# Score products of two heads side by side in the halves of the partitions: layer 0's attention of a two-block network

## The chip, the cores and the metric

The kernel runs on one core of a Trainium2 chip. The metric is the device time of one execution in microseconds (us), lower is better; it is given as the median of several runs. Names of engines in the rows: PE is TensorE's matmuls, PEld its weight loads, DVE is VectorE, ACT is ScalarE, POOL is GpSimd, SP issues most transfers.

## What is computed

Two transformer blocks in float32 on 256 latent tokens and 256 context tokens of 1024 features. The change touches the first layer's mixer alone. It has sixteen heads of 64 features: eight of kind A (a window of 128 keys around the query, two key heads shared by four query heads each, and a sink per head in the softmax's sum) and eight of kind B (a neighbourhood on the token grid, with a learnt bias by row and column distance). Latent queries see 256 latent and 256 context keys, context queries see the 256 context keys. Cut to what matters:

```python
o_a = window_attention(qa, ka, va, ka_c, va_c, a_sink)                  # 8 heads, kind A
o_b = neighbourhood_attention(qb, kb, vb, kb_c, vb_c, b_rpb, rows_n)    # 8 heads, kind B
y_lat = concatenate([o_a, o_b]) @ w_out
oa_c = ctx_self_attention(qa_c, ka_c, va_c, scale, a_sink)              # context queries
ob_c = ctx_self_attention(qb_c, kb_c, vb_c, scale)
y_ctx = concatenate([oa_c, ob_c]) @ w_out
```

## The kernel before

Every float32 operand of a large product is kept as two parts of a shorter form, `hi` and `lo`, and a product is three matmuls (`mm3`, lines 297 to 299: hi x hi, hi x lo, lo x hi). In the rows a score product therefore has three lines: L297, L298, L299.

The queries and keys of two heads, a pair, lie transposed in one tile [128, 512]: head e of the pair has the partitions 64 e to 64 e + 63, the columns are 256 latent and 256 context tokens. A latent score product of one head and one query tile of 128 contracts over 64 partitions and streams all 512 keys; a context product streams 256.

The work of layer 0 is written as Python generators that are emitted side by side. `weave` takes at each step the generator that is least far on, measured by the sum of its yields; `lead` stretches one's sum. A scheduler then puts each engine's instructions in an order, by the order of emission and by when it expects operands to be there, and each engine works through its own list. The weaves around the change are these:

```python
self.weave(self.qkvA(), ada0(1), lead=(1.0, 1.100))
self.weave(self.chain(self.qkvB(0), self.outproj0(0)), self.chain(self.attnA(0), self.attnA(1)), ada0(2), lead=(1.0, 1.000, 1.000))
self.weave(self.qkvB(1), self.attnB(0), lead=(1.0, 1.000))
self.weave(self.outproj12(), self.attnB(1), self.lat_norm(A[0], R), lead=(2.000, 1.0, 1.000))
```

`attnA` and `attnB` each hand two pairs to `attn`. It goes through (pair, latent or context, head): `scores` of one, then `weigh` of the one before. `scores` makes the two query tiles of one head (tile `sl` for the latent, one tile `sc` with both query tiles for the context), adds the window mask (L1140) or the bias (L1142), and calls `softmax`: maxima (L1051), the negated maximum `nm` (L1053, L1055), exponentials with their sums (L1057), the sink's share (L1060, L1061), reciprocal and scaling (L1062, L1064). `weigh` transposes the probabilities (`turn`, tile `pps`, copied to `PT`) and, after the pair's second head, multiplies by the values (`values`, tile `ov`) and cuts the result into `OT`. The last `attn` has `split`: the latent parts of both pairs come first, then the context parts, and `lat_norm` begins with the latent's last out-projection as soon as the latent parts are done.

`bias(h)` fetches the bias of a head of kind B with four small transfers from POOL's queue (L1171), adds the column mask on POOL (L1173), and has two buffers `bm`.

PSUM: the pool `ps_s` has two banks (tag `s`, which `sl` and `sc` use), `ps_a` three (in-projection `ip`, out-projection `op`, most `ov`), `ps_t` two for transposes and one more, `fil`. The probabilities `Pm` are [128, 2, 512] with two buffers.

Other names in the rows: `wh` and `wl` are the parts of the weight blocks, cut from `wr` (L185, L186); `xl`, `xc` the residual streams; `qh`, `ql` the parts of q; `adaps` the modulation's products.

## Time and profile before

| what | value |
|---|---|
| median of 3 runs | 1709.74 us |
| lowest and highest | 1708.4 and 1711.4 us |
| span of the profiled execution | 1706.0 us |
| TensorE matmuls busy | 1655.3 us, 97% of the span |
| TensorE weight loads busy | 1405.4 us, 82% |
| VectorE busy | 1130.2 us, 66% |
| ScalarE busy | 715.1 us, 42% |
| GpSimd busy | 218.4 us, 13% |
| mean granted TensorE clock | 0.988 of full speed |

The profiled execution is one run under the hardware profiler; the span goes from its first to its last instruction, and the runs' median lies 3.7 us above it. Matmuls are pipelined, so the duration of one holds time in which the next has begun: what a matmul costs TensorE is read from one start to the next. Two matmuls can also run at the same time, and their busy time counts once.

### The profile page before, as it was taken

Reading aid. Unit: us, or ns where it says so; the run is one execution under the profiler, and the core shown is the slowest. Engines: PE = TensorE matmul, PEld = TensorE weight load, DVE = VectorE, ACT = ScalarE, POOL = GpSimd, SP = SyncE. Lnnn points to the kernel's source line nnn. Section 1 sums busy time; section 2 is a strip of 40 time slices with the busy share of each in tenths; the row PEclk is TensorE's granted clock in tenths of the full one; section 3 lists DMA queues with packets and bytes.
Section 4 is the critical chain, followed back from the end, with each engine's and each line's share of the span. In section 5 each row is a group of like instructions: output and inputs, shape, how many; then the busy total and the mean of one; then the engine's idle time right before and its main releaser. Section 6 shows DMA issues by size and latency. Waiting matters only on the chain.

```text
span 1706.0 us, 30446 instructions
## 1 busy us (share of the span) xinstructions
PE 1655.3 (97%) x12256; PEld 1405.4 (82%) x12256; DVE 1130.2 (66%) x2156; ACT 715.1 (42%) x1336; POOL 218.4 (13%) x294
## 2 busy tenths in 40 slices
PE   7999999999999999998999999999999999999998
PEld 5676687687877787666667999998989999899997
DVE  3575856667767776558777885675865856665643
ACT  3344443332332323147664644443533435444442
POOL 1430132110000000225321100101020000100000
PEclk8999999999999999999999999999999999999999
DMA  9684254225567777573222454454423545545652
GB/s 339 210 230 126 53 58 72 54 83 185 179 210 239 243 245 221 161 232 107 67 58 64 147 163 146 152 172 116 139 73 112 157 132 159 173 139 184 185 168 81
DMA packets 193229, 257.31 MB, mean 151 GB/s; under 512 B 9263, under 2 KB 166816, under 8 KB 193088
## 3 DMA queue, kind: packets, MB, share of 16 engines
q1 hardware_dynamic: 189488, 248.29, 46.1%
q0 software_dynamic: 2016, 2.33, 3.0%
q10 hardware_dynamic: 1584, 4.74, 0.8%
q8 instruction: 96, 1.57, 0.4%
q14 instruction: 45, 0.37, 0.1%
HBM read 254.28 MB, written 1.05 MB: 150 GB/s over the span
## 4 chain that ended last, share of the span: by engine, by line
PE 89%; DMA 4%; ACT 2%; DVE 2%; issue 1%; POOL 1%; POOLq 0%; DVEq 0%; SPq 0%; ACTq 0%
PE m L297 11%; PE m L299 11%; PE m L298 11%; PE ov L1091 3%; PE pf L297 3%; PE pf L298 3%; PE pf L299 3%; PE ip L297 2%; PE ip L298 2%; PE ip L299 2%; PE pps L1077 2%; PE adaps L508 2%; PE part L362 2%; PE ml L1534 1%; PE pg L299 1%; PE pg L297 1%
## 5 line engine op out<-in xcount | busy, mean ns | idle before, releaser
L185 ACT ACTIVATE wh<-wr 128x1024 fp32r<-128x1024 f32 (+3 forms) x354 | 332.2, 984 | 420.9 <-PE m L298 189.9
L186 DVE TENSOR_TENSOR wl<-wr,wh 128x1024 fp32r<-128x1024 f32 (+3 forms) x354 | 402.2, 1164 | 146.6 <-ACT wh L185 145.9
L299 PE MATMUL m<-hh,wl 128*128 128x256 f32 (+1 forms) x544 | 177.5, 329 | 0.5 <-DVE wl L186 0.5
L297 PE MATMUL m<-hh,wh 128*128 128x256 f32 (+1 forms) x544 | 176.7, 330 | 1.1 <-ACT hh L395 1.1
L298 PE MATMUL m<-hl,wh 128*128 128x256 f32 (+1 forms) x544 | 177.1, 328 | 0.0
L297 PE MATMUL m<-hidh,wh 128*128 128x512 f32 (+1 forms) x512 | 173.6, 341 | 0.0
L298 PE MATMUL m<-hidl,wh 128*128 128x512 f32 (+1 forms) x512 | 172.6, 338 | 0.0
L299 PE MATMUL m<-hidh,wl 128*128 128x512 f32 (+1 forms) x512 | 172.6, 338 | 0.0
L357 POOL TENSOR_TENSOR sq<-xl 128x256 f32<-128x256 f32 x48 | 31.6, 662 | 721.1 <-DVE xl L1234 692.5
L299 PEld LDWEIGHTS m<-hh,wl 128*128 128x128 f32 x544 | 103.3, 190 | 11.6 <-issue 1.9
L297 PEld LDWEIGHTS m<-hh,wh 128*128 128x128 f32 x544 | 102.3, 190 | 12.6 <-issue 1.9
L298 PEld LDWEIGHTS m<-hl,wh 128*128 128x128 f32 x544 | 103.4, 190 | 9.5 <-issue 0.8
L297 PEld LDWEIGHTS m<-hidh,wh 128*128 128x128 f32 x512 | 96.7, 190 | 15.5 <-issue 3.8
L298 PEld LDWEIGHTS m<-hidl,wh 128*128 128x128 f32 x512 | 97.1, 190 | 14.6 <-issue 4.8
L299 PEld LDWEIGHTS m<-hidh,wl 128*128 128x128 f32 x512 | 96.9, 189 | 13.3 <-issue 3.3
L297 PE MATMUL pf<-hfh,wh 128*128 128x256 f32 x352 | 99.5, 287 | 1.1 <-ACT hfh L395 1.1
L298 PE MATMUL pf<-hfl,wh 128*128 128x256 f32 x352 | 100.0, 285 | 0.0
L299 PE MATMUL pf<-hfh,wl 128*128 128x256 f32 x352 | 100.0, 285 | 0.0
L297 PE MATMUL ip<-wh,hh 128*128 128x256 f32 x288 | 86.2, 301 | 0.0
L298 PE MATMUL ip<-wl,hh 128*128 128x256 f32 x288 | 84.6, 294 | 0.2 <-DVE wl L186 0.2
L299 PE MATMUL ip<-wh,hl 128*128 128x256 f32 x288 | 83.6, 290 | 0.0
L1234 DVE SCALAR_TENSOR_TENSOR xl<-m,mod,xl 128x256 f32<-128x256 f32 x64 | 30.6, 481 | 74.3 <-PE m L299 74.2
(592 smaller groups left out, 4185.2 us busy)
## 6 DMA issues: line engine op xcount, KB each, us to landing
wr<-in_mlp_w SPq DMA_DIRECT2D x128, 512.0 KB, 4.6
av<-in_ada_w SPq DMA_DIRECT2D x48, 512.0 KB, 4.0
wr<-in_w_ffn_in SPq DMA_DIRECT2D x44, 512.0 KB, 4.6
wr<-in_w_in SPq DMA_DIRECT2D x42, 512.0 KB, 4.4
wr<-in_ada_w SPq DMA_DIRECT2D x32, 512.0 KB, 6.2
av<-in_w_mod SPq DMA_DIRECT2D x32, 512.0 KB, 4.1
wr<-in_w_gate SPq DMA_DIRECT2D x24, 512.0 KB, 4.6
wf<-in_ada_w SPq DMA_DIRECT2D x16, 512.0 KB, 11.6
```

The lines of the kernel that those rows point to most:

```text
L185: b.nc.scalar.activation(out=hi[:, o + a:o + z], in_=t[:, a:z], func=AF.Copy)
L186: b.nc.vector.tensor_tensor(out=lo[:, o + a:o + z], in0=t[:, a:z], in1=hi[:, o + a:o + z], op=ALU.subtract)
L297: mm(ps, l.hi, r.hi, start=start, stop=False, **kw)
L298: mm(ps, l.hi, r.lo, start=False, stop=False, **kw)
L299: mm(ps, l.lo, r.hi, start=False, stop=stop, **kw)
L357: nc.gpsimd.tensor_tensor(out=d, in0=v, in1=v, op=ALU.mult)
L362: nc.tensor.matmul(part[j:j + 32, f], self.c1("ones"), sq[:, f], start=False, stop=c >= 3, skip_group_check=True)
L508: nc.tensor.matmul(ps[32 * j:32 * j + 32, :], S[:, k, :], m, start=k == 0, stop=k == KD - 1, skip_group_check=True)
L1077: nc.tensor.transpose(ps[:, o:o + P], pt[:, qt, k0:k0 + P], self.ident)
L1091: self.nc.tensor.matmul(o[64 * f:64 * f + 64, 0:256], vals(f, kt), T[f][:, kt, :], start=kt == 0, stop=kt == nk - 1, skip_group_check=True)
L1234: self.nc.vector.scalar_tensor_tensor(x, ps[:, 256 * i:256 * i + 256], mod[:, i, 8 * g + c:8 * g + c + 1], x, op0=ALU.mult, op1=ALU.add)
L1534: self.nc.tensor.matmul(s, q[:, i, t * P:t * P + P], k[:, i], start=True, stop=True)
```

## The change

The two heads of a pair are now scored together. `attn` goes through (pair, latent or context). A latent entry has two units, one for each query tile: `pair_scores` emits the three passes in turn, each for both heads, one on the lower and one on the upper 64 partitions, into one PSUM bank for each head. A context entry is one unit, with both query tiles and both heads in two banks. `softmax` takes a list of (scores, probabilities): two parts for a latent unit (two heads), four for a context unit. With a sink it now handles two heads of different sinks in one call, by operands that repeat a pair of columns, and the sink's share becomes an addition on VectorE and an exponential. The biases of both heads are fetched at the first query tile. `Pm` is [128, 512] with six buffers, of which a context head takes one. `weigh` runs for one head after each unit, as before, and for both after a context entry. The yields of the score products are half as many for a pair as before. The odd layer's call of `softmax` has a new form with the same instructions. Elsewhere the diff takes out comments.

```diff
@@ -1038,33 +1038,39 @@
         yield from self.inproj(1792 + 256 * g, post_v)
         yield from self.inproj(768 + 256 * g, post_n("q", v["b_q_norm"], True))
 
-    # -- layer 0: attention --
-    def softmax(self, S, n, scale, out, sink=None):
-        """out [128, 2, n] = softmax of the two query tiles scale * S[i] [128, n]; sink: (value, -value) [128, 1]."""
+    def softmax(self, parts, scale, sink=None):
         nc, sm = self.nc, self.small
-        mx = sm.tile([P, 2], F32, tag="mx", name="mx")
-        nm = sm.tile([P, 2], F32, tag="nm2", name="nm2")
-        su = sm.tile([P, 2], F32, tag="su", name="su")
-        parts = [slice(0, 2)] if self.in0 else [slice(0, 1), slice(1, 2)]
-        for c in parts:
+        n = len(parts)
+        mx = sm.tile([P, n], F32, tag="mx", name="mx")
+        nm = sm.tile([P, n], F32, tag="nm2", name="nm2")
+        su = sm.tile([P, n], F32, tag="su", name="su")
+        by = lambda t: t.rearrange("p (q e) -> p q e", e=2)
+        both = lambda t: t.unsqueeze(1).to_broadcast([P, n // 2, 2])
+        cols = [slice(0, n)] if self.in0 else [slice(i, i + 1) for i in range(n)]
+        for c in cols:
             for i in range(c.start, c.stop):
-                nc.vector.tensor_reduce(mx[:, i:i + 1], S[i], axis=AX.X, op=ALU.max)
+                nc.vector.tensor_reduce(mx[:, i:i + 1], parts[i][0], axis=AX.X, op=ALU.max)
             if sink is not None:
-                nc.vector.tensor_scalar(nm[:, c], mx[:, c], -scale, sink[1], op0=ALU.mult, op1=ALU.min)
+                nc.vector.scalar_tensor_tensor(by(nm), by(mx), -scale, both(sink[1]), op0=ALU.mult, op1=ALU.min)
             else:
                 nc.vector.tensor_scalar(nm[:, c], mx[:, c], -scale, None, op0=ALU.mult)
             for i in range(c.start, c.stop):
-                nc.scalar.activation(out=out[:, i, :n], in_=S[i], func=AF.Exp, scale=scale, bias=nm[:, i:i + 1], accum_out=su[:, i:i + 1])
+                nc.scalar.activation(out=parts[i][1], in_=parts[i][0], func=AF.Exp, scale=scale, bias=nm[:, i:i + 1],
+                                     accum_out=su[:, i:i + 1])
         if sink is not None:
-            es = sm.tile([P, 2], F32, tag="es", name="es")
-            nc.scalar.activation(out=es, in_=nm, func=AF.Exp, bias=sink[0])
+            es = sm.tile([P, n], F32, tag="es", name="es")
+            nc.vector.tensor_tensor(out=by(es), in0=by(nm), in1=both(sink[0]), op=ALU.add)
+            nc.scalar.activation(out=es, in_=es, func=AF.Exp)
             nc.vector.tensor_tensor(out=su, in0=su, in1=es, op=ALU.add)
         nc.vector.reciprocal(su, su)
-        for i in range(2):
-            nc.vector.tensor_scalar(out[:, i, :n], out[:, i, :n], su[:, i:i + 1], None, op0=ALU.mult)
+        for i, (_, out) in enumerate(parts):
+            nc.vector.tensor_scalar(out, out, su[:, i:i + 1], None, op0=ALU.mult)
 
     def turn(self, pt, n, act=0):
-        """P [128, 2, n] to P^T [128 keys, n / 128, 256 queries]."""
         nc = self.nc
         T = self.at3.tile([P, 4, 256], F32, tag="PT", name="PT", bufs=2 if self.in0 else 2)
         kt_n = n // P
@@ -1074,7 +1080,7 @@
                 for qt in range(2):
                     o = (kt * 2 + qt) * P
                     k0 = (2 * g + kt) * P
-                    nc.tensor.transpose(ps[:, o:o + P], pt[:, qt, k0:k0 + P], self.ident)
+                    nc.tensor.transpose(ps[:, o:o + P], pt[qt][:, k0:k0 + P], self.ident)
             dst, src = T[:, 2 * g:2 * g + 2], ps.rearrange("p (k q) -> p k q", k=2)
             if g and act < 2:
                 nc.vector.tensor_copy(dst, src)
@@ -1084,7 +1090,7 @@
         self.T = T
 
     def values(self, vals, T, nk, dst, back=False, own=False):
-        """dst Split [128, 256] = the outputs of the two heads, transposed; vals(e, kt) [128, 64]."""
         o = self.ps_t.tile([P, 512], F32, tag="fil", name="ov", bufs=1) if own else self.ps_a.tile([P, 512], F32, tag="a", name="ov")
         for kt in range(nk):
             for f in range(2):
@@ -1096,71 +1102,82 @@
             self.cut(dst, o[:, 0:256])
 
     def attn(self, pairs, OT, split=False):
-        """pairs: (q, k Split [128, 512], values(e, kt), heads, chunk of OT, kind)."""
-        todo = []
-        for pr in pairs:
-            for ctx in (False, True):
-                cell = {}
-                for e in range(2):
-                    todo.append((pr, e, ctx, cell))
+        todo = [(pr, ctx) for pr in pairs for ctx in (False, True)]
         if split:
-            todo.sort(key=lambda x: x[2])
+            todo.sort(key=lambda x: x[1])
+        old = None
         for i in range(len(todo) + 1):
-            if i < len(todo):
-                yield from self.scores(*todo[i])
-            if i > 0:
-                yield from self.weigh(*todo[i - 1], OT)
-                if split and i == 4:
-                    self.lat = True
-
-    def scores(self, pr, e, ctx, cell):
+            new = self.scores(*todo[i]) if i < len(todo) else ((), None)
+            for j in range(2):
+                if j < len(new[0]):
+                    yield from new[0][j]
+                if old:
+                    yield from self.weigh(*todo[i - 1], j, old, OT)
+            if split and i == 2:
+                self.lat = True
+            old = new[1]
+    def pair_scores(self, S, q, k, qs, ks):
+        rows = [slice(64 * e, 64 * e + 64) for e in range(2)]
+        for i, (a, b) in enumerate((("hi", "hi"), ("hi", "lo"), ("lo", "hi"))):
+            for e, r in enumerate(rows):
+                self.nc.tensor.matmul(S[e], getattr(q, a)[r, qs], getattr(k, b)[r, ks], start=i == 0, stop=i == 2)
+    def scores(self, pr, ctx):
         nc = self.nc
         q, k, vals, heads, chunk, kind = pr
-        rows = slice(64 * e, 64 * e + 64)
-        h = heads[e]
-        pt = self.at3.tile([P, 2, 512], F32, tag="P", name="Pm", bufs=2)
-        sink = (self.sink[:, h:h + 1], self.nsink[:, h:h + 1]) if kind == "A" else None
-        S = []
-        if ctx:
-            s = self.ps_s.tile([P, 2, 256], F32, tag="s", name="sc")
+        h = heads[0]
+        sink = (self.sink[:, h:h + 2], self.nsink[:, h:h + 2]) if kind == "A" else None
+        P_ = {}
+        tile = lambda: self.at3.tile([P, 512], F32, tag="P", name="Pm", bufs=6)
+        def both():
+            s = [self.ps_s.tile([P, 2, 256], F32, tag="s", name="sc") for _ in range(2)]
             for qt in range(2):
-                qs = slice(256 + qt * P, 256 + qt * P + P)
-                self.mm3(s[:, qt], q[rows, qs], k[rows, 256:512], True, True)
-            S = [s[:, 0], s[:, 1]]
-            n = 256
+                self.pair_scores([x[:, qt] for x in s], q, k, slice(256 + qt * P, 256 + qt * P + P), slice(256, 512))
             yield 0.8
-        else:
-            if kind == "B":
-                bm = self.bias(h)
-            for qt in range(2):
-                s = self.ps_s.tile([P, 512], F32, tag="s", name="sl")
-                self.mm3(s, q[rows, qt * P:qt * P + P], k[rows, 0:512], True, True)
+            for e in range(2):
+                t = tile()
+                for qt in range(2):
+                    P_[e, qt] = t[:, 256 * qt:256 * qt + 256]
+            self.softmax([(s[e][:, qt], P_[e, qt]) for qt in range(2) for e in range(2)], 0.125, sink)
+        def one(qt):
+            if kind == "B" and qt == 0:
+                P_["bias"] = [self.bias(x) for x in heads]
+            s = [self.ps_s.tile([P, 512], F32, tag="s", name="sl") for _ in range(2)]
+            self.pair_scores(s, q, k, slice(qt * P, qt * P + P), slice(0, 512))
+            yield 0.7
+            for e in range(2):
+                P_[e, qt] = tile()
                 if kind == "A":
                     o = slice(P, 2 * P) if qt == 0 else slice(0, P)
-                    nc.vector.tensor_tensor(out=s[:, o], in0=s[:, o], in1=self.c1("m0" if qt == 0 else "m1"), op=ALU.add)
+                    nc.vector.tensor_tensor(out=s[e][:, o], in0=s[e][:, o], in1=self.c1("m0" if qt == 0 else "m1"), op=ALU.add)
                 else:
-                    nc.vector.scalar_tensor_tensor(s[:, 0:256], bm[:, qt], 8.0, s[:, 0:256], op0=ALU.mult, op1=ALU.add)
-                S.append(s)
-                yield 0.7
-            n = 512
-        self.softmax(S, n, 0.125, pt, sink)
-        cell["P", e] = pt
-
-    def weigh(self, pr, e, ctx, cell, OT):
+                    nc.vector.scalar_tensor_tensor(s[e][:, 0:256], P_["bias"][e][:, qt], 8.0, s[e][:, 0:256], op0=ALU.mult, op1=ALU.add)
+            self.softmax([(s[e], P_[e, qt]) for e in range(2)], 0.125, sink)
+        return [both()] if ctx else [one(0), one(1)], P_
+    def weigh(self, pr, ctx, e, P_, OT):
         q, k, vals, heads, chunk, kind = pr
-        yield from self.turn(cell["P", e], 256 if ctx else 512)
-        cell["T", e] = self.T
-        if e == 1:
-            T = [cell["T", 0], cell["T", 1]]
-            if ctx:
-                self.values(lambda f, kt: vals(f, kt + 2), T, 2, OT[:, chunk, 256:512])
-                yield 0.9
-            else:
-                self.values(vals, T, 4, OT[:, chunk, 0:256], kind == "B")
-                yield 1.8
+        yield from self.turn([P_[e, qt] for qt in range(2)], 256 if ctx else 512)
+        P_["T", e] = self.T
+        if e == 0:
+            return
+        T = [P_["T", f] for f in range(2)]
+        if ctx:
+            self.values(lambda f, kt: vals(f, kt + 2), T, 2, OT[:, chunk, 256:512])
+            yield 0.9
+        else:
+            self.values(vals, T, 4, OT[:, chunk, 0:256], kind == "B")
+            yield 1.8
 
...
@@ -1535,10 +1552,11 @@
                     S.append(s)
                     yield 0.7
                 pt = self.at3.tile([P, 2, 512], F32, tag="P", name="Pl", bufs=3)
-                self.softmax(S, 512, sc, pt)
+                self.softmax([(S[t], pt[:, t]) for t in range(2)], sc)
                 Ps[i] = pt
             if i > 0:
-                yield from self.turn(Ps.pop(i - 1), 512, 2)
+                pt = Ps.pop(i - 1)
+                yield from self.turn([pt[:, t] for t in range(2)], 512, 2)
                 Ts[i - 1] = self.T
                 if i % 2 == 0:
```

## Rows read from the trace of the kernel before

**Rows 1.** The page, the chain that ended last, shares of the span by engine.

```profile
PE 89%; DMA 4%; ACT 2%; DVE 2%; issue 1%; POOL 1%; POOLq 0%; DVEq 0%; SPq 0%; ACTq 0%
```

**Rows 2.** Busy time by stretch; PE, PEld, DVE, ACT, POOL, clock, DMA share, GB/s.

```profile
135.00:187.00 52.00, 51.69 (x336) 37.77 (x333) 34.24 (x89) 23.36 (x59) 2.92 (x1) 1.00 0.29 96
187.00:206.00 19.00, 16.42 (x93) 11.81 (x91) 16.03 (x43) 9.74 (x28) 0.00 (x0) 1.00 0.02 6
206.00:281.00 75.00, 74.31 (x500) 60.96 (x500) 43.18 (x98) 31.83 (x72) 20.97 (x22) 1.00 0.49 70
281.00:335.00 54.00, 50.76 (x269) 35.57 (x268) 36.87 (x91) 18.73 (x47) 11.84 (x18) 0.94 0.39 49
```

**Rows 3.** The chain, 118 to 136 us; start, us, what.

```profile
118.81 15.93 DMA wr<-in_ada_w
```

**Rows 4.** The chain, 187 to 206 us.

```profile
188.50 0.84 ACT qh L319 x2
```

**Rows 5.** POOL in order of time; start, duration, line, operation, count [idle before].

```profile
114.05 5.01 POOL L1171 DMA_DIRECT2D bm<-in_b_rpb  x8
...
133.89 1.09 POOL L1173 TENSOR_TENSOR bm<-bm,cst 128x512 f32<-128x512 f32 x1 [6.67 <-DMA bm<-in_b_rpb]
...
284.22 2.47 POOL L1171 DMA_DIRECT2D bm<-in_b_rpb  x4 [9.85 <-DVE sl L1142]
294.94 1.08 POOL L1173 TENSOR_TENSOR bm<-bm,cst 128x512 f32<-128x512 f32 x1 [8.25 <-DMA bm<-in_b_rpb]
...
305.24 1.09 POOL L1173 TENSOR_TENSOR bm<-bm,cst 128x512 f32<-128x512 f32 x1 [6.83 <-DMA bm<-in_b_rpb]
```

**Rows 6.** TensorE in order of time: a latent triple and what follows it.

```profile
151.56 0.50 PE L297 MATMUL sl<-kh,qh 64*128 64x512 f32 x1
...
152.47 0.44 PE L1091 MATMUL ov<-PT,vA 128*64 128x256 f32 x2
```

**Rows 7.** TensorE: two latent triples back to back and what follows.

```profile
281.44 0.49 PE L297 MATMUL sl<-kh,qh 64*128 64x512 f32 x1
...
283.02 0.50 PE L297 MATMUL op<-OTh,wh 128*128 128x512 f32 x1
```

**Rows 8.** TensorE: the context scores of a pair and what follows.

```profile
145.81 0.38 PE L297 MATMUL sc<-kh,qh 64*128 64x256 f32 x1
...
146.38 0.29 PE L298 MATMUL sc<-kl,qh 64*128 64x256 f32 x2
146.50 0.29 PE L299 MATMUL sc<-kh,ql 64*128 64x256 f32 x2
...
147.06 0.38 PE L298 MATMUL ip<-wl,hh 128*128 128x256 f32 x1
```

**Rows 9.** Busy time by stretch of what touches `sl`; PE, PEld, DVE, ACT.

```profile
135.00:187.00 52.00, 7.69 (x24) 3.83 (x24) 7.88 (x16) 4.35 (x12) 1.00 0.29 96
...
206.00:281.00 75.00, 7.40 (x24) 3.90 (x24) 8.69 (x16) 5.79 (x16) 1.00 0.49 70
```

**Rows 10.** The same of what touches `sc`.

```profile
135.00:187.00 52.00, 2.64 (x24) 2.22 (x24) 2.84 (x8) 4.09 (x16) 1.00 0.29 96
...
206.00:281.00 75.00, 3.88 (x24) 3.07 (x24) 3.08 (x8) 4.16 (x17) 1.00 0.49 70
```

**Rows 11.** VectorE in order of time, 281 to 312 us.

```profile
282.89 0.76 DVE L1142 SCALAR_TENSOR_TENSOR sl<-bm,sl 128x256 f32<-128x256 f32 x2 [0.48 <-PE sl L299]
...
299.16 0.43 DVE L1142 SCALAR_TENSOR_TENSOR sl<-bm,sl 128x256 f32<-128x256 f32 x1
...
307.03 1.22 DVE L186 TENSOR_TENSOR wl<-wr,wh 128x1024 fp32r<-128x1024 f32 x1
...
311.42 0.16 DVE L1055 TENSOR_SCALAR nm<-mx 128x2 f32<-128x2 f32 x1
```

**Rows 12.** ScalarE in order of time: the first exponential behind it.

```profile
285.08 0.69 ACT L1057 ACTIVATE Pm<-sl,nm 128x512 f32<-128x512 f32 x1 [4.75 <-DVE nm L1055]
```

**Rows 13.** DMA queues, 283 to 307 us; packets, MB, share of sixteen engines.

```profile
q0 software_dynamic: 256, 0.52, 57.5%
```

## The prediction

> **What bounds the kernel now.** I read the page's chain of work first: 89% of the span is TensorE [rows 1], so whatever shortens TensorE's stream can shorten the program, but only where the chain runs through TensorE. The change touches layer 0's attention alone, all of it ahead of 335 us. I cut that part where the program's weaves change or the chain leaves TensorE, and read each stretch by windows [rows 2]: 135 to 187 us (TensorE busy 51.69 of 52.00), 187 to 206 (16.42 of 19.00, with VectorE at 16.03), 206 to 281 (74.31 of 75.00) and 281 to 335 (50.76 of 54.00, granted clock 0.94). The reader is to see two full stretches and two that are not full.
>
> Then I asked the chain what the gaps are. Before 135 us it stands 15.93 us on one load of ada_w [rows 3]. From 188.5 us it runs over ScalarE and VectorE, beginning with the cut of q [rows 4]. From 283 us it runs through the bias of the last two heads: four small transfers, their landing, an addition on POOL, four more, their landing, an addition [rows 5]. Only in the two full stretches is TensorE time taken out of the program with certainty.
>
> **The change, part by part.** *Score products, latent.* Before, a query tile of one head takes three passes of 512 columns on 64 partitions: 151.56 to 152.47 us, 0.91 us with the switch into and out of the 64-row form [rows 6]; two query tiles back to back take 281.44 to 283.02, 1.58 us [rows 7]. After, three passes serve two heads if the two halves of the partitions run side by side. The trace of before already has such a place: from 145.81 us the two heads' context scores, twelve passes, lie partly across each other. At 146.38 and 146.50 us two instructions each run as a pair, one pair 0.12 us after the other; the twelve give way after 1.25 us [rows 8], where nine steps of 0.118 (three pairs, six single) and 0.2 of switches make 1.26 and twelve would make 1.6. So a pair costs a pass. I carry that over to 512 columns, where no row shows it; the bounds there are 0.91 us a pair (side by side) and 1.58 us (one after the other, as back to back).
>
> 135 to 187 us: 24 matmuls `sl` [rows 9] are eight triples of 0.91 = 7.28 us and become four groups of 0.91 = 3.64 us: 3.6 us saved. 206 to 281 us: again 24, but busy 0.29 us less [rows 9], as two of the eight stand back to back: 1.58 + 6 x 0.91 = 7.04 us become 3.64: 3.4 us saved.
>
> *Score products, context.* Per pair twelve passes of 256 columns become six steps. Where the heads already overlap for three steps, 1.25 - 3 x 0.118 = 0.90 us remains and 0.35 is saved: two pairs in 135 to 187, 0.7 us. In 206 to 281 the same 24 matmuls keep TensorE busy 3.88 us instead of 2.64 [rows 10], because the heads stand apart: 1.24 and those 0.7 make 1.9, less 0.1 for the ends of matmuls that other work covers: 1.8 us saved.
>
> The Trainium skill, "TensorE: Matmul & The Clock Gate", section "LDWEIGHTS (loading the stationary operand)", gives a weight load as columns / 1.2 ns, 107 ns for 128 columns; two loads one after the other would make a paired pass of 256 columns 0.21 us, and by it the sum's context terms would shrink by 24 x 0.095 = 2.3 us. The pairs of [rows 8] are 0.12 us apart, so here the loads go side by side too, which is what that page's Part 3 says of tiles in different row groups.
>
> *Softmax.* A call takes two heads of one query tile instead of two tiles of one head; the context call takes four parts. The large operations stay as many: a maximum, an exponential and a scaling for each head and query tile. The small ones on VectorE, around 0.16 us like the negation of [rows 11]: a pair of kind A has 4 calls x 3 before, 3 calls x 4 after (the addition of the sink to the shift is new); a pair of kind B 4 x 2 before, 3 x 2 after. I cost this at nothing: in the two full stretches VectorE is busy 34.24 of 52 and 43.18 of 75 us [rows 2], and that slack hides it; without it the four A pairs pay a dearer negation, well under 1 us in all.
>
> *The two score banks.* One unit now holds both buffers of `s`, and the next unit's first pass needs both free. From the end of the scores to the exponentials the rows take 282.89 to 285.08 us [rows 11, 12], two exponentials of 0.69 follow: 3.6 us, 4.5 with the scores. Before, a latent head also held both. A pair has three such units, 13.5 us, while the full stretches have 26 and 37 us for a pair: hidden by in-projection matmuls.
>
> *The bias.* It is fetched for both heads of a pair at once, into two buffers that come free only when both query tiles of the pair before have been added. In the weave at 206 us the second pair comes some 20 us after that, about what the fetch takes; I cost it at nothing, and at 2 us if that cover is gone. In the last weave the latent parts of the two pairs follow each other directly, and the chain hangs on the bias already. Worked out with S = 281.4, the start of the first scores [rows 7]: both score tiles end at S + 1.05; additions, maxima, negation 2.2 us, exponentials 1.4: banks free at S + 4.7. The second tile's scores can begin there; before, 2.2 us more passed, so S + 4.7 to 6.9, and I take 6.0. Its additions end 1.8 us later, at S + 7.8, POOL begins 0.6 us after. Then eight transfers: the eight of this stretch took 57.5% of sixteen DMA engines' 24 us [rows 13], 13.8 us, so with 1.9 us of issue and 1.1 of addition at least 16.8; issued in two turns with an addition between, as from 284.22 us, 22.1 us; the batch of eight at 114.05 us, beside weight loads, took 20.9 [rows 5]. I take 19, between them: ready at S + 27.4 = 308.8 us, against 306.3 now. But then two units are left instead of one: 3.6 us to the end of the first exponentials, 1.05 of scores, 2.3 to the second negation give 315.8, against 311.6 now [rows 11]: 4.2 us later. Behind it the transposes of one head more wait (1.0 us), and the context scores are 2.2 us shorter. Net 3.0 us lost in this stretch; the ends are 10 us lost (6.9, 22.1, and two weight cuts of 1.22 us within the chain, as at 307.03 us now [rows 11]) and 1.6 gained (4.7, 16.8).
>
> *Not counted.* The stretch before 135 us frees about 3.6 us of TensorE (three pairs of query tiles and a context pair), which goes into waiting for ada_w; 187 to 206 us frees 1.0, where the chain is on VectorE and ScalarE.
>
> **Sum.** 3.6 + 0.7 + 3.4 + 1.8 = 9.5 us saved, 3.0 lost: 6.5 us. The profiled execution's 1706.0 us would become 1699.5; it lies 3.7 us under the median 1709.74, which becomes 1703.2.
>
> **Rivals.** *All of it arrives.* The bias is ready no later than now, and the last two stretches yield too: 9.5 + 1.0 + 5.0 = 15.5 us, 1694. For it: TensorE is nearly always busy. Against: [rows 5] put the last stretch on the bias. Chance 0.12.
>
> *Another engine sets the pace.* With both banks in one unit and VectorE at 16 of 19 us before 206 us, TensorE's saved time becomes waiting for softmax; or the change doesn't do what it says, 512-column halves run one after the other, and 4 x 1.58 instead of 8 x 0.91 saves 1 us a stretch. The gain falls to 0 to 3 us: 1707 to 1712. Chance 0.23.
>
> *The bias chain costs more than the scores give.* Slower than before: the second pair's fetch takes 22.1 us behind a late release, ready at S + 31.4, while VectorE, which works in order, has the second pair's first addition queued at S + 18, where the third head's stands now (299.16 us) [rows 11]. Then it stands for 13 us, the out-projection's residual additions behind it wait, the three `a` buffers fill with chunks of 2.75 us (twelve passes of 0.23) and TensorE loses another 5 or 6 us: 10 + 6 lost against 9.5 gained, 1716. It decides from a loss of 12.9 us in the last stretch. Chance 0.15.
>
> The forecast keeps 0.50, with its own range 1699 to 1707.
>
> **How the numbers follow.** About 0.2%, 3.4 us, can be told from no change. Faster: 0.12 and nearly all of 0.50, 0.60; same: the second rival and the edge of the forecast, 0.24; slower 0.16. The range runs into the cases on both sides, 1695 to 1713, which leaves out most of the first and of the third rival.
>
> **What would show it.** Right: `sl` matmuls starting in pairs, three steps of 0.23 us; 135 to 187 and 206 to 281 us shorter by 4 and 5 us at a busy TensorE; in the last weave eight bias transfers in a row, an addition on VectorE waiting for POOL, and TensorE idle near 310 us. Wrong: the two matmuls of a pass 0.23 us apart; TensorE waiting for exponentials in the full stretches; a later stretch of the program that differs.

## The result and the profile after

The changed kernel takes 1725.0 us, the median of four runs (1722.7 to 1726.0), beside 1709.7 us for four of the kernel before on the same chip: the ratio is 1.009, with a 95% interval of 1.0076 to 1.0104. It is slower by 15 us. Forecast were 1703.2 us and a range up to 1713. The profiled execution went from 1706.0 to 1723.3 us.

First the page: TensorE's share of the chain, which was 89% [rows 1], and the granted clock in 40 slices of 43 us.

```profile
PEclk8999998899999999998999999999999999999999
...
PE 90%; DMA 3%; DVE 3%; ACT 2%; issue 1%; POOL 1%; POOLq 0%; DVEq 0%; SPq 0%; ACTq 0%
```

TensorE is still the chain, but two slices from 258 to 345 us, and one in layer 1, are at 8, beside the first. So I cut the program at marks that both kernels have (the first latent scores, the last in-projection matmul, the first MLP matmul, the first and the last of layer 1) and read each piece by windows; the columns are those of [rows 2]. Of before, three pieces: scores to in-projection, the last weave, layer 1.

```profile
93.70:269.30 175.60, 169.88 (x1121) 127.57 (x1121) 113.18 (x286) 77.40 (x194) 35.06 (x42) 1.00 0.46 100
269.30:344.50 75.20, 71.96 (x395) 51.78 (x393) 51.40 (x122) 26.91 (x63) 18.18 (x24) 0.95 0.36 64
...
736.30:918.90 182.60, 173.41 (x982) 122.29 (x982) 132.14 (x355) 117.40 (x288) 52.77 (x77) 1.00 0.30 94
```

The same three of after:

```profile
93.80:268.10 174.30, 168.22 (x1124) 124.64 (x1124) 112.16 (x282) 75.66 (x191) 34.74 (x42) 0.98 0.46 101
268.10:354.30 86.20, 75.17 (x392) 53.34 (x390) 52.18 (x118) 26.18 (x61) 18.41 (x24) 0.84 0.26 55
...
746.00:936.00 190.00, 179.82 (x985) 127.05 (x983) 130.39 (x352) 117.72 (x287) 50.91 (x77) 0.96 0.29 91
```

The pieces between and behind them differ by at most 0.5 us. So 1.3 us were won in the first, 11.0 lost in the last weave and 7.4 lost in layer 1, whose code makes the same instructions as before. Both losing pieces have a lower granted clock. The clock has two levels here, 2.4 GHz and half of it, so a mean of 0.84 over 86.2 us says that some 27 us ran at half (2 x 0.16 x 86.2); before it were some 7. In layer 1 it was none before and some 15 us after. Over the three pieces together TensorE's idle time grew by 9.1 us and its busy time by 8.0, though the pairs take work out of it.

The loss begins with TensorE's waits. The view of waits of after, 94 to 354 us (line, what it waited for, us in total, times, longest):

```profile
PE sc L1126 <- ACT Pm L1061: 5.4, 1, 5.4
PE sl L1126 <- ACT Pm L1061: 5.2, 2, 3.1
PE pps L1083 <- DVE Pm L1070: 2.8, 2, 2.2
```

Of before, 94 to 345 us, the largest and the only one for scores:

```profile
PE ov L1091 <- ACT PT L1082: 3.9, 7, 1.5
...
PE sc L297 <- ACT Pm L1057: 0.6, 1, 0.6
```

TensorE now waits 10.6 us for exponentials, the last readers of the two score banks, and 2.8 us for VectorE's scaling of the probabilities. Where the longest waits lie, TensorE in order of time shows (start, duration, what, idle before and its releaser):

```profile
167.80 1.06 PE L1083 MATMUL pps<-cst,Pm 128*128 128x128 f32 x6 [2.21 <-DVE Pm L1070]
...
288.73 0.79 PE L1126 MATMUL sl<-kh,qh 64*128 64x512 f32 x1 [3.12 <-ACT Pm L1061]
...
293.77 0.79 PE L1126 MATMUL sl<-kh,qh 64*128 64x512 f32 x1 [2.11 <-ACT Pm L1061]
...
318.59 0.58 PE L1126 MATMUL sc<-kh,qh 64*128 64x256 f32 x1 [5.40 <-ACT Pm L1061]
```

And windows show what follows them:

```profile
168.30:175.10 6.80, 6.02 (x23) 3.46 (x22) 4.91 (x15) 3.10 (x12) 0.00 (x0) 0.50 0.01 2
...
281.00:287.80 6.80, 4.61 (x22) 2.95 (x20) 6.20 (x12) 2.01 (x2) 0.00 (x0) 1.00 0.36 112
287.80:301.40 13.60, 10.45 (x30) 6.59 (x31) 5.04 (x14) 4.08 (x10) 6.15 (x9) 0.50 0.67 56
301.50:315.10 13.60, 11.69 (x59) 7.87 (x58) 8.40 (x19) 3.83 (x7) 1.09 (x1) 1.00 0.06 5
315.20:328.70 13.50, 10.00 (x45) 7.97 (x45) 7.74 (x21) 4.35 (x14) 0.00 (x0) 0.50 0.26 78
```

Full clock until TensorE has stood idle; half of it within or behind the wait; full again; half again at the next wait. The first row's wait lies in the first of the forecast's two full stretches; before, TensorE hardly waited there and its clock was full [rows 2]. In the last weave of before, the clock was half once, for 6.8 us:

```profile
311.60:318.40 6.80, 6.11 (x30) 4.60 (x31) 3.96 (x13) 3.67 (x13) 0.00 (x0) 0.50 0.25 77
```

Why the waits in the last weave are this long, VectorE in order of time shows at the first and the last of them, and between them at the third unit's first addition of the bias:

```profile
284.94 0.75 DVE L1160 SCALAR_TENSOR_TENSOR sl<-bm,sl 128x256 f32<-128x256 f32 x2
...
286.20 0.47 DVE L1251 SCALAR_TENSOR_TENSOR xl<-op,mod,xl 128x256 f32<-128x256 f32 x1
286.59 0.47 DVE L1251 SCALAR_TENSOR_TENSOR xc<-op,mod,xc 128x256 f32<-128x256 f32 x1
...
287.70 0.17 DVE L1059 TENSOR_SCALAR nm<-mx 128x2 f32<-128x2 f32 x1
...
301.39 0.43 DVE L1160 SCALAR_TENSOR_TENSOR sl<-bm,sl 128x256 f32<-128x256 f32 x1 [3.11 <-POOL bm L1190]
...
314.18 2.35 DVE L186 TENSOR_TENSOR wl<-wr,wh 128x1024 fp32r<-128x1024 f32 x2
...
317.50 0.17 DVE L1059 TENSOR_SCALAR nm<-mx 128x2 f32<-128x2 f32 x1
```

The first pair's scores begin at 283.75 us, and the next unit begins at 288.73, 5.0 us later, when the first of the two banks is free; its second head follows 0.7 us behind. Two residual additions stand between the maxima. Ahead of the context scores two weight cuts stand in the same place, 2.35 us, and from the scores of the unit before, at 311.00, to these 7.6 us pass.

The bias, which the forecast feared, on POOL (compare [rows 5]):

```profile
291.41 5.06 POOL L1188 DMA_DIRECT2D bm<-in_b_rpb  x8 [18.19 <-DVE sl L1160]
300.27 1.09 POOL L1190 TENSOR_TENSOR bm<-bm,cst 128x512 f32<-128x512 f32 x1 [3.80 <-DMA bm<-in_b_rpb]
304.21 1.09 POOL L1190 TENSOR_TENSOR bm<-bm,cst 128x512 f32<-128x512 f32 x1 [2.85 <-DMA bm<-in_b_rpb]
```

Eight transfers in a batch, ready 13.9 us after the first issue, at 305.3 us: earlier than before (306.3), not later. But the bias still holds things up. The third unit's scores begin at 293.77 us and get their two additions only at 301.39 and 305.33, so both banks are held until 309.3; the fourth unit begins at 311.00, and the context scores behind it at 318.59. Before the change no latent unit stood between the bias and the context scores, and these began 6.1 us earlier:

```profile
312.51 0.58 PE L297 MATMUL sc<-kh,qh 64*128 64x256 f32 x1 [0.58 <-ACT Pm L1057]
```

Last, the scores themselves. A pair that stands together, and one that the planner took apart, with an in-projection matmul between:

```profile
122.53 0.49 PE L1126 MATMUL sl<-kh,qh 64*128 64x512 f32 x1
...
123.42 0.38 PE L298 MATMUL ip<-wl,hh 128*128 128x256 f32 x1
123.73 0.49 PE L1126 MATMUL sl<-kh,qh 64*128 64x512 f32 x1
...
183.48 0.50 PE L1126 MATMUL sl<-kh,qh 64*128 64x512 f32 x2
183.82 0.40 PE L1126 MATMUL sl<-kl,qh 64*128 64x512 f32 x2
184.05 0.40 PE L1126 MATMUL sl<-kh,ql 64*128 64x512 f32 x2
184.38 0.65 PE L1083 MATMUL pps<-cst,Pm 128*128 128x128 f32 x4
```

Six matmuls from 183.48 to 184.38, 0.90 us, what three cost before [rows 6]. But three alone still cost 0.89 (122.53 to 123.42), and of the twelve latent units of the first piece six were taken apart.

### The profile page after: what moved, and what is told of

Read it like the earlier page. It is cut to its first block, busy times and chain, and to the rows that moved or that the text cites. A ratio compares the mean times of both kernels' runs of the same rounds, so it can differ in the third digit from the quotient of the medians.

```text
span 1723.3 us, 30425 instructions
## 1 busy us (share of the span) xinstructions
PE 1662.8 (96%) x12256; PEld 1407.9 (82%) x12256; DVE 1130.2 (66%) x2148; ACT 712.7 (41%) x1332; POOL 217.6 (13%) x294
## 4 chain that ended last, share of the span: by engine, by line
PE 90%; DMA 3%; DVE 3%; ACT 2%; issue 1%; POOL 1%; POOLq 0%; DVEq 0%; SPq 0%; ACTq 0%
PE m L297 11%; PE m L299 10%; PE m L298 10%; PE ov L1097 3%; PE pf L297 3%; PE pf L298 2%; PE pf L299 2%; PE ip L297 2%; PE pps L1083 2%; PE ip L298 2%; PE ip L299 2%; PE adaps L508 2%; PE ml L1551 1%; PE part L362 1%; PE pg L299 1%; PE pg L297 1%
## 5 line engine op out<-in xcount | busy, mean ns | idle before, releaser
L297 PE MATMUL ip<-wh,hh 128*128 128x256 f32 x288 | 86.2, 301 | 0.0
L551 DVE SCALAR_TENSOR_TENSOR acc<-av,S,acc 128x1024 f32<-128x1024 f32 x56 | 70.6, 1280 | 13.9 <-DMA av<-in_ada_w 13.7
```

The lines of the kernel that those rows point to most:

```text
L297: mm(ps, l.hi, r.hi, start=start, stop=False, **kw)
L551: op = eng.scalar_tensor_tensor(d, w, s, d, op0=ALU.mult, op1=ALU.add)
```

## Experiments

Lengths below are those of the three pieces above in the profiled execution, in this order: first piece, last weave, layer 1. The measured time of each kernel is a median, with its ratio to the kernel before on the same chip. Executions of one kernel lie 3 to 12 us apart, and the profiled one need not be near the median: it took 1733.6 us beside 1727.3 for the pairs in the last weave only, 1731.1 beside 1722.0 for one head after the other, 1722.8 beside 1718.0 for the two edits together.

### Where: the last weave alone, and all but it

Two kernels keep the scores of the kernel before in one part of layer 0.

```diff
-        yield from self.attn(pairs, self.OT[2 + g], g == 1)
+        yield from (self.attn_old if g == 1 else self.attn)(pairs, self.OT[2 + g], g == 1)
```

> The changed kernel, but the last weave's attention (heads 4 to 7 of kind B) goes head by head as before the change. If the last weave alone carries the loss of layer 0, its stretch from the last in-projection to the first matmul of the MLP is 75 to 78 us instead of 86, and the whole is 1709 to 1716 us, less if layer 1 also comes back to 183 us. If the loss is spread over the weaves, 1718 to 1724.

Measured 1715.9 us, ratio 1.0025 (1.0011 to 1.0038); 176.5, 81.9 and 185.9 us: the whole as expected, the weave longer. The other way round, pairs in the last weave only:

```diff
-        yield from self.attn(pairs, self.OT[g])
+        yield from self.attn_old(pairs, self.OT[g])
...
-        yield from self.attn(pairs, self.OT[2 + g], g == 1)
+        yield from (self.attn if g == 1 else self.attn_old)(pairs, self.OT[2 + g], g == 1)
```

> The mirror image: only the last weave's attention is paired, the three others go head by head. If the last weave alone carries the loss of layer 0, its stretch is 83 to 88 us and the whole 1716 to 1723 us. If the loss comes from elsewhere, the stretch is 75 to 79 us and the whole 1707 to 1713.

Measured 1727.3, ratio 1.0088 (1.0067 to 1.011); 185.8, 84.9 and 188.1 us. With pairs in it alone the last weave is nearly as long as in the change, and without them 9 of the 15 us are gone; the whole time lies above both ranges. But even the weave with the old scores takes 81.9 us instead of 75.2, with a clock of 0.90, and a first piece with the old scores takes 185.8 instead of 175.6, with a clock of 0.94. Both kernels keep the new form of the softmax and of its tiles, and in both the planner orders everything anew; which of the two costs this, no run tells.

### The bias

The last pair takes the bias tiles of the pair before and fetches none.

```diff
-                P_["bias"] = [self.bias(x) for x in heads]
+                if h != 6:
+                    self.bias_tiles = [self.bias(x) for x in heads]
+                P_["bias"] = self.bias_tiles
```

> The changed kernel, but the last pair of kind B (heads 6 and 7) adds the bias tiles of heads 4 and 5 and fetches none of its own, so that its bias is there at once; left out: these two heads' own bias. Theory 'bias' (the late fetch in the last weave makes the loss): VectorE's waits of 3.1 and 2.8 us for POOL near 301 and 305 us go, the units behind move up, 1717 to 1720 us. Theory 'banks' (each unit holds both score banks, TensorE stands for exponentials at 285, 291 and 313 us and its clock falls): those waits stay, 1722 to 1726 us.

Measured 1711.4, ratio 1.0017 (1.0002 to 1.0031); 173.2, 76.1 and 186.0 us: below both ranges. Its waits from 266 to 350 us:

```profile
PE sl L1126 <- ACT Pm L1061: 5.2, 2, 3.1
```

The waits of 3.1 and 2.1 us stayed, that of 5.4 us ahead of the context scores went, and with it 10 us: the fourth unit begins 10.8 us after the third, instead of 17.2. So far the late bias could be the whole cause of that wait. The next run speaks against that.

### The context's two banks

The context scores go back to one head and one bank at a time, each with its own softmax; the bias stays as in the change.

```diff
-            s = [self.ps_s.tile([P, 2, 256], F32, tag="s", name="sc") for _ in range(2)]
+            s = self.ps_s.tile([P, 2, 256], F32, tag="s", name="sc")
...
-                self.pair_scores([x[:, qt] for x in s], q, k, slice(256 + qt * P, 256 + qt * P + P), slice(256, 512))
+                self.mm3(s[:, qt], q[r, 256 + qt * P:256 + qt * P + P], k[r, 256:512], True, True)
...
-        return [both()] if ctx else [one(0), one(1)], P_
+        return [ctx1(0), ctx1(1)] if ctx else [one(0), one(1)], P_
```

> The changed kernel, but the context scores stay as before the change, a unit for each head with one bank and its own softmax; the latent units stay paired. Theory 'banks': the wait of 5.4 us ahead of the context scores near 313 us shrinks since one free bank is enough, and part of the half clock behind it goes, 1716 to 1721 us. Theory 'bias': within 3 us of the changed kernel, 1722 to 1728.

Measured 1707.3, ratio 0.9987 (0.9977 to 0.9996): 18 us under the change, below both ranges, and level with before. Windows of its three pieces:

```profile
92.00:266.90 174.90, 171.15 (x1120) 127.65 (x1120) 113.91 (x302) 75.45 (x194) 34.94 (x42) 0.97 0.43 100
266.90:345.40 78.50, 72.65 (x398) 50.56 (x396) 51.13 (x118) 27.02 (x61) 19.18 (x26) 0.96 0.29 61
737.10:918.90 181.80, 172.34 (x985) 123.53 (x983) 131.51 (x355) 117.17 (x288) 52.30 (x77) 0.99 0.30 95
```

The bias is fetched as in the change, and the weave is nearly as short as before, at a clock of 0.96. What this run and the one ahead of it share is that the wait before the context scores is gone. Either edit removes it, so neither the late bias nor the two banks of the context makes it alone.

### The weights of the planner's order

The change halves the yields of the score units. Three kernels turn that: yields doubled in the change (1.4 and 1.6), halved in the kernel before (0.35 and 0.4), and the first together with the context head by head (1.4 and 0.8).

> The changed kernel, but a score unit counts for the weave what two heads' units counted before (1.4 for a query tile, 1.6 for a context unit), so that twice as much other work is put between two units. Theory 'banks': the waits of 3.1, 2.1 and 5.4 us shrink and with them the time at half clock, 1710 to 1719 us. Theory 'bias': within 3 us of the changed kernel, 1722 to 1728, because the fetch starts as late.

Measured 1710.5, ratio 0.9997 (0.9985 to 1.0009); 170.6, 81.5 and 180.0 us. In the last weave TensorE waits 6.0 us for exponentials instead of 10.6, as expected; but of the time that came back 3.7 us lie in the first piece, 4.7 in the weave and 10.0 in layer 1.

> The kernel before the change, but its score units count half for the weave (0.35 for a query tile, 0.4 for a context unit), as they do after the change; nothing else of the change. Theory 'weights' (it is the halved weight that bunches the units): TensorE waits for exponentials and the last weave grows from 75 to 80 us or more, 1715 to 1722 us. Theory 'banks' (it is that a unit of two heads holds both banks to the end of its softmax): 1706 to 1713.

Measured 1717.8, ratio 1.0037 (1.0027 to 1.0047); 178.2, 78.2 and 184.5 us. The time is that of the theory 'weights', not its mechanism: TensorE waits 0.2 us for exponentials in the last weave.

> The changed kernel with latent units that count 1.4 for the weave and context units for each head with one bank: the two edits that took the loss back, together. Theory 'banks': the side-by-side latent passes now show as gain, the stretch of the first scores to the last in-projection 170 to 172 us and the last weave 75 to 79, 1699 to 1707 us. If the planner's order of layer 1 decides the total, anywhere from 1700 to 1715 with layer 1 between 180 and 190 us.

Measured 1718.0, ratio 1.0049 (1.003 to 1.0067); 174.0, 85.9 and 183.8 us: above both ranges. The doubled yields and the context head by head each brought the change level with before; together they lost half of it again, and the clock of the last weave, 0.90 and 0.96 by themselves, is 0.88. The halved yields alone cost the kernel before some 7 us. Effects of single edits don't add up here, since each makes a new order of the program.

### Side by side or one after the other

The passes of the first head, then those of the second, in the order of emission.

```diff
-        for i, (a, b) in enumerate((("hi", "hi"), ("hi", "lo"), ("lo", "hi"))):
-            for e, r in enumerate(rows):
+        for e, r in enumerate(rows):
+            for i, (a, b) in enumerate((("hi", "hi"), ("hi", "lo"), ("lo", "hi"))):
```

> The changed kernel, but a unit emits all passes of the first head and then those of the second, so that nothing runs side by side by design. If the side-by-side passes yield what was forecast and TensorE bounds the stretches, eight latent units of 0.9 us become 1.6 and the context units 1.5, some 8 to 10 us more: 1733 to 1735. Theory 'banks': part of that time is waiting anyway, 1725 to 1731.

Measured 1722.0, ratio 1.0079 (1.0049 to 1.0109); 178.8, 86.2 and 190.1 us: below both ranges. The edit did not do what it was made for. In TensorE's list the three passes of one head stand ahead of the three of the other, and yet they ran like this:

```profile
154.54 0.51 PE L1126 MATMUL sl<-kh,qh 64*128 64x512 f32 x2
154.88 0.40 PE L1126 MATMUL sl<-kl,qh 64*128 64x512 f32 x2
155.11 0.40 PE L1126 MATMUL sl<-kh,ql 64*128 64x512 f32 x2
155.44 0.44 PE L1097 MATMUL ov<-PT,vA 128*64 128x256 f32 x2
```

Six in 0.90 us. It says nothing on the worth of running side by side; that took the next runs.

### The pairs held together

The order of each unit's matmuls is fixed: the first waits for the exponentials that read the banks last, and the passes of the two heads follow each other.

```diff
+                if prev is not None:
+                    self.tc.add_manual_dep(m.ins, prev.name, mybir.DependencyInfo(kind, mybir.DependencyReason.DATA), reason="pair")
+                prev, kind = m.ins, mybir.DependencyClass.NoSync
```

> The changed kernel with the order of each pair's score matmuls fixed: the first waits until both banks are free, and the passes of the two heads follow each other by turns, in all 24 units but for two that other work splits once. Theory, a pair costs a pass where it stands together: six matmuls take 0.9 us instead of 1.2 to 1.8 in the 11 latent units that the planner took apart, and the context's 12 take 0.9 to 1.25; 4 to 8 us less TensorE work in all, of which the first stretch (174.3 us from the first scores to the last in-projection matmul) gives 2 to 5: 169 to 172, without its half clock 168 to 170. The last weave keeps its waits and its half clock, 80 to 88 us. Whole time 1716 to 1724. Rival, both banks at once cost more than the passes give: TensorE waits longer ahead of each unit, more half clock in the first stretch, 175 to 182 there, whole time 1725 to 1735.

Measured 1710.1, ratio 0.9987 (0.9975 to 0.9999). Its first two pieces, and below them what touched `sl` in the first piece of this kernel:

```profile
93.40:263.30 169.90, 159.57 (x1125) 119.39 (x1125) 109.28 (x282) 75.08 (x191) 36.23 (x42) 0.98 0.45 103
263.30:348.70 85.40, 72.47 (x392) 50.59 (x391) 50.75 (x114) 26.10 (x60) 19.13 (x26) 0.88 0.26 56
...
94.00:263.30 169.30, 12.16 (x70) 5.88 (x66) 21.82 (x48) 17.48 (x48) 0.98 0.45 103
```

The latter was 17.61 us in the change:

```profile
94.00:268.10 174.10, 17.61 (x72) 8.67 (x72) 23.26 (x48) 17.35 (x48) 0.98 0.46 101
```

and in the kernel before

```profile
94.00:269.30 175.30, 22.22 (x72) 11.44 (x71) 24.17 (x48) 17.38 (x48) 1.00 0.46 100
```

Held together, the pairs give what was forecast of them: 10.1 us of TensorE's score work (70 of the 72 matmuls are in the trace). The 11 units of the expectation are six here; in the last weave there are two more whose heads start 0.7 us apart. All of TensorE's work in the piece went from 169.9 to 159.6 us, and the piece from 175.6 to 169.9: 5.7 us arrived, and the rest became waiting (10.3 us not busy, 5.7 before). The last weave stayed at 85.4, where the theory had it; layer 1 took 180.6 us, which neither theory had counted, and so the time came out 6 us under the theory's.

The same with the context head by head:

> As the run before it for the latent units, but the context scores head by head in one bank each, with a softmax of their own (the form that took 1707.3 without the fixed order). Theory, the passes pay and the context's two banks are what made TensorE wait ahead of the context scores: first stretch 168 to 172, last weave 75 to 80, layer 1 180 to 186, whole time 1699 to 1707, under both kernels. Rival, holding the pair's passes back until both banks are free makes new waits: 1708 to 1720.

Measured 1717.6, ratio 1.0032 (1.0019 to 1.0044); 176.0, 85.7 and 179.0 us: the rival's time, with a wait of 5.2 us ahead of the context scores after all. So one bank for each head doesn't remove that wait in every order. And with the last weave as before the change:

> The pairs with the fixed order up to the last weave, and the last weave head by head as before the change (1715.9 without the fixed order). Theory, the pairs cost only where no long in-projection matmuls stand beside them: first stretch 168 to 172, last weave 72 to 80, whole time 1700 to 1710. Rival, the planner's order of the rest and the clock decide, whatever the form: first stretch 172 to 180, whole time 1710 to 1722.

Measured 1713.8, ratio 1.0011 (1.0002 to 1.0021); 170.9, 80.0 and 184.6 us. The first piece came as expected, the weave at its upper end, and the sum missed by 4 us.

### The clock: matmuls that nothing reads

If half clock behind the waits is the loss, TensorE must be faster when it has useless work in the waits. Five lots of eight matmuls of 128x512 go ahead of the later score units of the last weave of the change; their results are not read.

```diff
+    def busy(self, q, k, h, kind):
+        if kind == "B" and h >= 4:
+            o = self.ps_a.tile([P, 512], F32, tag="a", name="busy")
+            for _ in range(8):
+                self.nc.tensor.matmul(o, q.hi[:, 0:P], k.hi[:, 0:512], start=True, stop=True)
```

> The changed kernel with 40 matmuls of 128x512 added whose result nothing reads, in five lots of eight ahead of the second and later score units of the last weave (heads of kind B from 4 up); all the kernel's own work stays. At the mean of the two triples shown before the change (1.58 us for six, 0.26 each) they are 10.5 us of TensorE work. Theory, the granted clock: the waits for the exponentials (3.1, 2.1 and 5.4 us in the changed kernel) are partly filled, TensorE idles less, its clock stays up, and the stretch from the last in-projection matmul to the first of the MLP, 86.1 us with 27.3 of them at half clock, comes out no longer than 84 (76 to 84), with under 17 us at half clock, though work was added. Rival, the waits themselves set the stretch: the matmuls fill at most the waits, the half clock stays where it is, and the stretch takes 86 or more, up to 96 if they stand ahead of what others wait for. The rest of the kernel may move by some 5 us, because the planner orders it anew: whole time 1712 to 1726 by the theory, 1724 to 1736 by the rival.

Measured 1715.5, ratio 1.0027 (1.0016 to 1.0037): 9.5 us less than the change, with 10.6 us of work more; 177.2, 83.9 and 180.1 us. The last weave by windows, and the part of the added matmuls in it:

```profile
270.70:354.60 83.90, 78.39 (x433) 55.38 (x431) 50.59 (x114) 26.07 (x60) 19.11 (x26) 1.00 0.28 57
...
270.70:354.60 83.90, 10.58 (x40) 7.29 (x40) 1.00 0.28 57
```

The half clock is gone altogether, from some 27 us to none, and the weave is 2.3 us shorter with 10.6 us more in it. The kernel's own work there keeps TensorE busy 67.8 us (78.39 less 10.58) instead of 75.2, and the idle time is 5.5 us instead of 11.0: the lots took waits and half clock away together. Most of the gain in the whole time lies in layer 1, as that came out 9.9 us shorter, and is no proof of this. The control is the kernel before, with five such lots:

> A control: the kernel before the change with the same kind of matmuls, five lots of eight in the last weave (heads of kind B from 5 up, and the context scores of heads 4 and 6), 10.5 us at 0.26 each. There TensorE waits only some 3 us in this weave and has 6.8 us at half clock. Theory, the granted clock: at most those 3.4 us come back, so the lots cost most of what they take: the weave takes 79 to 86 instead of 75.2, whole time 1713 to 1721. Rival, such lots help for another reason (by the planner's order, whatever the waits): the weave is no longer than before, whole time 1705 to 1711.

Measured 1710.3, ratio 1.0004 (0.999 to 1.0018). The weave took 79.3 us instead of 75.2:

```profile
270.10:349.40 79.30, 78.75 (x435) 56.89 (x433) 52.23 (x123) 27.65 (x64) 18.15 (x24) 1.00 0.33 60
```

There is little to win there, and the lots cost 4.1 of their 10.5 us: 2.7 went into idle time (3.2 us before, 0.5 now), and most of the rest can be the 6.8 us at half clock that are gone. The rival, a weave no longer than 75.2, fell. The whole time did not follow, as layer 1 was 3.7 us shorter, at full clock in both; that part of the theory's expectation missed. Three lots on the pairs held together:

> The fixed order of the pairs, and ahead of the three units of the last weave that waited (3.8, 3.2, 3.0 us) a lot of eight matmuls of 128x512 that nothing reads, 24 in all, 6.3 us at 0.26 each. Theory, the granted clock: the half clock of the last weave falls from 20.5 us to under 7, which gives back some 7 us, and the lots lie in waits of 10 us that are there anyway: the weave takes 75 to 80 instead of 85.5, whole time 1699 to 1706, under both kernels, though work was added. Rival, the lots add what they take: 86 to 92, whole time 1709 to 1718.

Measured 1708.3, ratio 0.9985 (0.9974 to 0.9997); 169.4, 82.8 and 180.5 us, clock of the weave 0.96 instead of 0.88. In the theory's direction, but 2.6 us won instead of 5 to 10: two waits of 3.6 and 2.3 us stayed, ahead of the scores at 290.97 and 304.77 us, and the planner had put the lots at 270.46, 275.82 and 306.69.

### The pace of the out-projection

The work that could fill the waits is the out-projection of heads 4 to 11. The weave's lead makes it run ahead; here less so, with the pairs held together.

```diff
-            self.weave(self.outproj12(), self.attnB(1), self.lat_norm(A[0], R), lead=(2.000, 1.0, 1.000))
+            self.weave(self.outproj12(), self.attnB(1), self.lat_norm(A[0], R), lead=(1.400, 1.0, 1.000))
```

> The fixed order of the pairs as in the run that took 1710.1, and in the last weave the out-projection of heads 4 to 11 spread over 1.4 instead of 2.0 of the other work's pace (its number in the lead of the last weave), so that less of it is used up before the waits. Theory, the waits of the last weave are holes that the planner could fill with matmuls which stand ready: the three waits (3.8, 3.2 and 3.0 us without it) shrink to under 6 us in all, the half clock of the last weave falls under 11 us, and the weave takes 76 to 81 instead of 85.5: whole time 1700 to 1707, under both kernels. Rival, the pace does not decide, since each pair waits for the softmax of the pair before it whatever stands around it: 83 to 88 in the last weave, whole time 1707 to 1716.

Measured 1706.2, ratio 0.9972 (0.9959 to 0.9985): the fastest of all, 19 us under the change and 4 under the kernel before. By windows, the first two pieces:

```profile
92.00:263.40 171.40, 160.05 (x1125) 119.67 (x1125) 109.39 (x282) 75.05 (x191) 36.27 (x42) 0.97 0.45 102
263.40:344.20 80.80, 68.50 (x391) 47.53 (x390) 51.67 (x118) 26.40 (x61) 18.39 (x24) 0.92 0.28 59
```

The weave is 4.6 us shorter and its clock is up from 0.88 to 0.92, but the reason that was given holds only in part: TensorE still waits 10.8 us for exponentials there (9.2 and 1.6). Neither they nor the half clock fell as far as expected. What changed is that two waits follow each other from 277.9 us, with one stretch at half clock behind them instead of two apart.

## Why the prediction was wrong

**A pair costs a pass: right.** Six matmuls take 0.90 us instead of 1.8, and with all pairs together TensorE spends 10.1 us less on the latent scores of the first piece. The "3.6 us saved" and "3.4 us saved" of the two full stretches were right as work. They failed as forecast of this kernel: six of the twelve units were taken apart, since the two banks come free one after the other and the planner emits what is ready; 4.6 us of the 10.1 came.

**"Hidden by in-projection matmuls": the step that failed.** The forecast cost the two score banks at nothing. Its time from the first score to free banks, S + 4.7, was near: 5.0 us to the first bank twice, 7.6 where two weight cuts came in. What failed is the cover. The sentence looked at the full stretches, where in-projection matmuls hide this; in the last weave, where what could hide it was used up or not ready, TensorE stood idle for 3.1, 2.1 and 5.4 us, and no term of the sum but the bias asked for it. The same happened once on a smaller scale in a full stretch, to the softmax that VectorE's slack was to hide: 2.2 us of waiting, 6.8 us at half clock behind it, and from 135 to 187 us a TensorE that is busy 49.01 of 52 us.

**No term for the clock.** A wait was priced at its length. In the last weave TensorE's idle time grew by 7.8 us (3.2 to 11.0) and its busy time by 3.2 (72.0 to 75.2). The busy time holds the work at half clock. With useless matmuls and no half clock the kernel's own work took 67.8 us, 7.4 less than in the change, and that of the kernel before 68.5 (78.75 less 10.29 of added matmuls), 3.5 less. So by estimate some 4 of the 11.0 us are the clock and 7.8 the idle time, less 0.7 us of work; the runs with useless matmuls have another order of the work too, so the split is rough. The four executions of the kernel with pairs in the last weave only, the same program each time, point the same way: 1733.6, 1728.7, 1726.0 and 1722.9 us at mean clocks of 0.976, 0.979, 0.980 and 0.981. What the runs give for the clock as cause, besides this, is that useless matmuls in the waits took all of the half clock away and made the weave shorter, while in the control, where there is hardly a wait, they made it longer. The Trainium skill, "TensorE: Matmul & The Clock Gate", section "Terms", prices throttled time at its length times the share of the clock that is lacking: by it an estimate of some 13.7 us for the 27.3 here. The runs show the 7.4; TensorE is idle in a quarter of that time (busy 20.45 of 27.1 us in the two windows at 0.50). Its section "A second HAM failure mode: psum-queue depth-cycling" describes a kernel whose TensorE stands still for moments as it cycles through PSUM banks, so that the clock goes up and down; the windows around 288 and 315 us show a clock that goes down and up here too, behind waits of 2.1 to 5.4 us for the score banks.

**The bias: right that it stays on the path, wrong in its times.** It was forecast ready 19 us after the issue, at least 16.8, and 2.5 us later than before. It was ready after 13.9 us and 1.0 us sooner. VectorE waited 3.1 and 2.8 us for it. But one unit more stands behind it, as the forecast says, and that unit took 6.7 us from its scores to its negation (311.00 to 317.67) instead of 3.4, since VectorE had residual additions and two weight cuts to do between. So the forecast's 4.2 us, net 3.0, came out as 6.1 at the context scores, although the fetch was quicker. The ends of this term, "10 us lost" and "1.6 gained", don't come out of its own figures, which give 9.4 and 0.5. The rival "The bias chain costs more than the scores give" had the sign and 6 of the 15 us, by a VectorE standing for 13 us that didn't happen; what did is the "two weight cuts of 1.22 us within the chain", between maximum and exponential. Leaving the fetch out takes the wait ahead of the context scores away, and so does the context head by head with the full fetch: the bias is one of two conditions, not the cause by itself.

**"The change touches layer 0's attention alone": the second step that failed.** Layer 1 had no term, so it was held at 0, and it cost 7.4 us. Over the 17 kernels profiled it took between 178.9 and 190.1 us with the same instructions; only their order and the granted clock (0.96 to 1.00) differ. The order decides most of it: kernels whose TensorE goes through layer 1 in the same order, read as groups of like instructions, are alike, whatever the edit. The change, one head after the other and the pairs in the last weave only share one order and took 190.0, 190.1 and 188.1 us; two others took 186.0 and 185.9, four 180.0 to 181.8, two 179.0 and 178.9. All kernels above 184 us have a clock under 1.00 there. In the change each of the four stretches at half clock begins 0.4 to 1.7 us behind a wait of 1.6 to 2.4 us. What in the order makes the clock fall is not settled: before, waits of 2.2 and 1.6 us have no half clock behind them, and the waits that the trace names in layer 1 are much the same before and after (for the key transposes 2.4 and 3.3 us, for the compressed keys 2.2 and 2.4).

**The range.** 1695 to 1713 was made of costs in places where the change works. The planner's new order alone moves the kernel by several us: halved yields alone made the kernel before 7 us slower, and two edits that each recover 14 us or more recover 7 together. That belonged in the range, on both sides.

## What to carry to other kernels

Holding all buffers of a kind in one unit is free only where other work of the same engine is left to be emitted; look for the last stretch, and add up what VectorE does between the scores and the release, its other duties included. A wait of TensorE of some us was paid twice here, as idle time (7.8 us in the last weave) and again as half clock (some 4 us of slower work, by the estimate above), so price waits without cover at more than their length, here about one and a half times, and see whether pending work can be spread into them. Where a planner orders the program, an edit's own effect can be smaller than that of the new order: read pieces of the program that the edit doesn't touch, and fix the order of what must stand together.

## What the hardware showed that was not expected

Matmuls of two heads on different halves of the partitions ran side by side also where the three of one head stand ahead of the three of the other in TensorE's list (154.54 to 155.44 us in that run, six in 0.90 us). So the order within a unit didn't matter here; what mattered is that no matmul on all 128 partitions stands between the heads (with an in-projection matmul between, each three took 0.89 us).

Forty matmuls, 10.6 us of TensorE's work, added to a stretch of 86.2 us made it 2.3 us shorter.
